# Attention probabilities of the second block: scaling by gate over denominator moved from VectorE to ScalarE, one step later

## The chip, the cores and the metric

One core of one Trainium2 chip runs the whole program. The metric is the time of one execution in microseconds (us) of device time; lower is better. The engines are TensorE (PE, with its weight loads shown apart as PEld), VectorE (DVE), ScalarE (ACT), GpSimd (POOL) and SyncE (SP). Each runs its own instructions in a fixed order and waits on semaphores for the others.

## What is computed

Two transformer blocks, one after the other, on 512 tokens of width 1024 in float32. The change lies in the second one, a sparse-attention mixer with 16 heads of 64 and three gated branches. Two of them, "selected" and "window", are the `br` 0 and 1 of the code. With 512 tokens both are ordinary causal attention with a bias by distance:

```
gates = sigmoid(g)                      # one per token, branch and head
logits = q @ k.T * dh ** -0.5 + bias    # (head, query, key)
p = masked_softmax(logits, dist >= 0)
o = p @ v
y = sum over branches of gates * o * silu(z)
...
h = x + rms_norm(y @ w_out)
```

So each row of probabilities may be multiplied by gate / denominator before it meets the values: both factors are one number per query and head.

## The kernel before, in words

All large products are made of three float32r products (high times high, low times high, high times low); weights are split into a high part by ScalarE (`wh`, line 172) and a low part by VectorE or, in the last part of the program, by GpSimd (`wl`, line 174).

The attention of the second block (function `attention`, about 960 to 1330 us of the span) has 128 steps: 8 pairs of heads, 2 branches, 2 heads of the pair, 4 blocks `tb` of 128 queries. Step k does this for its head and block, with n = 128, 256, 384 or 512 keys:

- `scores` (lines 1173 to 1182): PE makes the scores S in one of two PSUM banks that take turns (`sc`, banks 2 and 3). VectorE adds the bias in place and finds the row's extreme `nm` (line 1176). ScalarE takes the exponential into P, 128xn in SBUF, and sums it into `rd` (line 1180). VectorE takes the reciprocal of `rd` (line 1181) and multiplies P by `rd` and by the gate column in `gn`, in place (line 1182; the trace shows it as L295, the helper `ts`).
- `flip`, three steps later (`LAG` is 2): PE transposes P's blocks (line 1195) into one of two PSUM banks (`tp`, banks 4 and 5); ScalarE copies out the high part (`ptall`, line 1198), VectorE the low part (line 1199, shown as L301, the helper `tt`).
- `mix`, after every second flip and two steps later: PE multiplies by the values (line 1211); at a head's end ScalarE and VectorE move the sum out (`t`, lines 1217 and 1218).

P has one buffer for each `tb`, so step k+4 writes the buffer that step k's flip has read. Between these parts, `fill.run` issues pieces of other work on PE: the projections of keys, queries and of z (lines 341 to 343), and the compressed branch, whose 64 additions F_ on VectorE (line 910, shown as L301) fall in the first 100 us. `ns` sets how much by a budget of estimated PE time.

The order of instructions on PE and GpSimd is the program's (`manual_schedule`). On VectorE and ScalarE a scheduler sets the order when the program is built, by its own estimates of when each instruction can start.

Of the kernel before, what the change touches and what calls it, by code (L numbers as in the profile page):

```python
# [10 lines left out]
AF = mybir.ActivationFunctionType  # L11
OP = mybir.AluOpType
# [241 lines left out]
def tile_blocks(ctx, tc, x, xt, wts, prm, cst, table, post_g, w2k, w2v, out):  # L254
    nc = tc.nc
    v, s, g, pe, sy = nc.vector, nc.scalar, nc.gpsimd, nc.tensor, nc.sync
# [31 lines left out]
    def small(shape, name, bufs=2):  # L288
        return glob.tile(shape, F32, name=name, tag=name, bufs=bufs)

    def ts(out_, in_, s1, s2=None, op0=OP.mult, op1=None, eng=None):
        if s2 is None:
            (eng or v).tensor_scalar(out_, in_, s1, None, op0)
        else:
            (eng or v).tensor_scalar(out_, in_, s1, s2, op0, op1)  # L295
# [4 lines left out]
    def tt(out_, a, b, op=OP.mult, eng=None):  # L300
        (eng or v).tensor_tensor(out_, a, b, op)  # L301
# [478 lines left out]
    def nsa(x2, ssq2):  # L780
# [4 lines left out]
        with ExitStack() as pts:  # L785
# [46 lines left out]
            gn = pn.tile([128, 4, 48], F32, name="gn")  # L832
# [196 lines left out]
            def load_near(gq):  # L1029
                P = glob.tile([128, 16, 32], F32, name="Pc", tag="rb", bufs=1)  # L1030
                sy.dma_start(P.rearrange("p (t r) c -> p t r c", t=4), cb_d[:, :, 4 * gq:4 * gq + 4, :])
                pct["p", gq] = P

            def cmp_scores(gq, half):
                P = pct["p", gq]
                S = mx()
                used[0] = opened[0]
                for i in range(2):
                    for r in range(4):
                        t0 = 256 * half + 128 * i  # L1040
                        pe.matmul(S[:, 256 * i + 64 * r:256 * i + 64 * r + 64], qst[4 * gq + r][:, t0:t0 + 128],
                                  kc[:, gq].rearrange("p a b -> p (a b)"), start=True, stop=True)
                S4 = S.rearrange("p (a l b) -> p a l b", l=2, b=32)
                Ph = P[:, 8 * half:8 * half + 8, :]
                for l in range(2):
                    tt(Ph, S4[:, :, l, :], Ph, OP.add)

            def cmp_shift(gq):
                P = pct["p", gq]
                mns = small([128, 16], "mns")  # L1050
                v.tensor_reduce(mns, P, AX.X, OP.min)
                tt(P, P, mns[:, :, None].to_broadcast([128, 16, 32]), OP.subtract)
# [108 lines left out]
            class Unit:  # L1161
# [5 lines left out]
                def scores(self, tb):  # L1167
                    h, br = self.h, self.br
                    kh, kl = kst[h // 4, br]
                    n = 128 * tb + 128  # L1170
                    S = sc()
                    q = qst[h][:, 128 * tb:128 * tb + 128]
                    pe.matmul(S[:, 0:n], q, kh[:, 0:n], start=True, stop=False)
                    pe.matmul(S[:, 0:n], q, kl[:, 0:n], start=False, stop=True)
                    nm = small([128, 1], "nm", 4)
                    v.tensor_tensor_reduce(S[:, 0:n], S[:, 0:n], self.bt[:, h % 2, 512 - n:512], 1.0,  # L1176
                                           -NEG, OP.add, OP.min, nm)
                    P = pt.tile([128, n], F32, name="P", tag=f"P{tb}", bufs=1)
                    rd = small([128, 1], "rd", 4)
                    latest[0] = s.activation(P[:, 0:n], S[:, 0:n], AF.Exp, bias=nm, scale=-1.0, accum_out=rd)  # L1180
                    v.reciprocal(rd, rd)
                    ts(P[:, 0:n], P[:, 0:n], rd, gn[:, tb, 16 * br + 16 + h:16 * br + 17 + h], OP.mult, OP.mult)
                    self.P[tb] = P

                def flip(self, tb):
                    n = 128 * tb + 128
                    half, i = divmod(tb, 2)
                    if i == 0:
                        self.PT[half] = (ptall[:, turn[0], 0], ptall[:, turn[0], 1])
                        turn[0] = 1 - turn[0]  # L1190
                    PTh, PTl = self.PT[half]
                    P = self.P.pop(tb)
                    pst = tp()
                    for sb in range(tb + 1):
                        pe.transpose(pst[:, 128 * sb:128 * sb + 128], P[:, 128 * sb:128 * sb + 128], ident)  # L1195
                    src = pst[:, 0:n].rearrange("p (a b) -> p a b", b=128)
                    hi = PTh[:, 0:tb + 1, 128 * i:128 * i + 128]
                    s.copy(hi, src)
                    tt(PTl[:, 0:tb + 1, 128 * i:128 * i + 128], src, hi.bitcast(F32), OP.subtract)
# [18 lines left out]
                        tt(self.t1[a, :], self.t1[a, :], o[b, :], OP.add)  # L1218

            def attention(fill):  # L1220
                pend_flip, pend_mix = [], []
                steps = 128
                tick = [0]
                for p in range(1, 8):
                    fill.add(combine(p), 15600.0)
                    if p == 2:
                        fill.add(queries(6), 5200.0)
                    if p == 3:
                        fill.add(keys(3), 5200.0)
                    if p == 4:  # L1230
                        fill.add(queries(7), 5200.0)

                def mixes(limit=MLAG):
                    if len(pend_mix) > 0 and (tick[0] >= pend_mix[0][2] + limit):
                        u, half, _ = pend_mix.pop(0)
                        u.mix(half)
                        if u.h % 2 == 1 and u.br == 1 and half == 1:
                            attended(u.h // 2, u.ots)

                def flips(limit):  # L1240
                    if len(pend_flip) > limit:
                        u, tb = pend_flip.pop(0)
                        u.flip(tb)
                        if tb % 2 == 1:
                            return [(u, tb // 2, tick[0])]
                    return []

                bts = []
                bt2 = [pt.tile([128, 2, 512], F32, name="bt", tag=f"bt{i}", bufs=1) for i in range(2)]
                for bt in bt2:  # L1250
                    v.memset(bt[:, :, 0:256], 0.0)

                def load_bias(p):
                    bt = bt2[p % 2]
                    base = bt_d[2 * p:2 * p + 2]
                    sy.dma_start(bt[:, :, 256:512], bass.AP(tensor=base.tensor, offset=base.offset + 127,
                                                            ap=[[383, 128], [128 * 384, 2], [1, 256]]))
                    bts.append(bt)

                load_bias(0)  # L1260
                for p in range(8):
                    while p >= 2 and not {(p - 2, 1), (p - 2, 2)} <= joined:
                        fill.ticks += 1
                        assert fill._job() or fill._step() or fill.ticks < 9999
                    while (p // 2, 1) not in kst or 2 * p + 1 not in qst:
                        assert fill._step()
                    bt = bts.pop(0)
                    ots = []
                    for br in range(2):
                        t1 = pt.tile([128, T], F32, name="t1", tag="ot", bufs=4)  # L1270
                        ots.append(t1)
                        for e in range(2):
                            u = Unit(2 * p + e, br, bt, t1)
                            u.ots = ots
                            for tb in range(4):
                                steps -= 1
                                tick[0] += 1
                                ns = FILL if p < 2 else fill.left / (steps + TAIL)
                                u.scores(tb)
                                fill.run(ns / 2)  # L1280
                                new = flips(LAG)
                                fill.run(ns / 2)
                                mixes()
                                pend_mix += new
                                pend_flip.append((u, tb))
                            if br == 0 and e == 1 and p < 7:
                                load_bias(p + 1)
                while pend_flip or pend_mix:
                    tick[0] += 1
                    new = flips(0)  # L1290
                    fill.run(ns)
                    mixes()
                    pend_mix += new
# [114 lines left out]
```

## Time and profile before

| | |
|---|---|
| median of 3 runs | 1399.81 us (1399.77 to 1400.01) |
| the profiled execution | 1398.81 us, its span 1397.1 us |
| PE busy | 1337.3 us (96%) |
| VectorE busy | 808.5 us (58%) |
| ScalarE busy | 650.6 us (47%) |
| GpSimd busy | 261.2 us (19%) |
| mean granted clock of PE | 0.99 of full speed |

The shares are means over stages that differ. In the rows below a line such as L295 is a line of the kernel, often a helper's, `out<-in` names the tiles, and an engine's idle time is put down to the instruction that released it. "Busy" of PE contains modelled ends, so a busy PE is not PE at its peak.

### The profile page before, as it was taken

The page shows a single profiled execution, that of the slowest core. Times are in us where ns is not written, and L with a number is a line of the kernel's source. Part 1 is how long each engine was busy: PE and PEld are TensorE (multiplying, and loading weights), DVE is VectorE, ACT ScalarE, POOL GpSimd, SP SyncE. Part 2 cuts the span into 40 slices and gives each one's busy share as a digit, 9 for nine tenths or more (in the row PEclk, how much of TensorE's full clock was granted, in tenths as well). Part 3 has the DMA queues.
Part 4 walks back from the last instruction along what each step waited for, and adds up shares of the span by engine and source line. Part 5 has one row for each costly group of instructions (what it writes and reads, how often), then busy time and mean ns, then how long its engine had stood idle before and what let it go on. Part 6 is the DMA issues. An engine that isn't in the chain of part 4 may idle for free.

```text
span 1397.1 us, 17790 instructions
## 1 busy us (share of the span) xinstructions
PE 1337.3 (96%) x6622; PEld 1090.3 (78%) x6622; DVE 808.5 (58%) x1596; ACT 650.6 (47%) x1273; POOL 261.2 (19%) x230
## 2 busy tenths in 40 slices
PE   9999999999999999989999999899788999999897
PEld 7977787778786888868888888788677878777776
DVE  4678535556667535232233323455988998988823
ACT  6577624443434325341135422254446656665522
POOL 0022101111101000000000000134536242333352
PEclk9999999999999999999999999999999999999999
DMA  7411121213131414843333323314223122121132
GB/s 232 137 46 47 61 91 61 91 49 103 46 106 46 154 57 142 110 166 92 100 94 93 104 91 121 125 50 130 75 71 106 54 61 61 53 68 46 55 121 76
DMA packets 42039, 125.31 MB, mean 90 GB/s; under 512 B 4528, under 2 KB 11232, under 8 KB 41696
## 3 DMA queue, kind: packets, MB, share of 16 engines
q1 hardware_dynamic: 41952, 124.17, 29.4%
q8 instruction: 52, 0.85, 0.2%
q14 instruction: 35, 0.29, 0.1%
HBM read 115.77 MB, written 8.39 MB: 89 GB/s over the span
## 4 chain that ended last, share of the span: by engine, by line
PE 59%; DVE 16%; issue 15%; ACT 6%; POOL 2%; DMA 1%; SPq 0%; POOLq 0%; DVEq 0%; ACTq 0%
PE b L375 9%; PE b L374 9%; PE b L376 9%; PE b L341 8%; PE b L343 8%; PE b L342 8%; DVE P L295 4%; DVE b L1176 2%; DVE ptall L301 2%; ACT wh L172 1%; PE b L827 1%; ACT P L1180 1%; PE b L1211 1%; PE b L544 1%; PE b L1195 1%
## 5 line engine op out<-in xcount | busy, mean ns | idle before, releaser
L172 ACT CAST wh<-wr 128x1024 fp32r<-128x1024 f32 (+3 forms) x204 | 207.6, 1020 | 385.9 <-PE b L376 222.7
L341 PE MATMUL b<-ah,wh 128*128 128x512 f32 x808 | 330.5, 409 | 6.3 <-ACT wh L172 5.9
L174 DVE TENSOR_TENSOR wl<-wr,wh 128x1024 fp32r<-128x1024 f32 (+2 forms) x142 | 169.2, 1194 | 281.1 <-ACT wh L172 280.7
L343 PE MATMUL b<-ah,wl 128*128 128x512 f32 x808 | 318.9, 395 | 0.6 <-DVE wl L174 0.5
L342 PE MATMUL b<-al,wh 128*128 128x512 f32 x808 | 318.2, 394 | 0.0
L343 PEld LDWEIGHTS b<-ah,wl 128*128 128x128 f32 x808 | 152.8, 189 | 35.4 <-DVE wl L174 1.8
L341 PEld LDWEIGHTS b<-ah,wh 128*128 128x128 f32 x808 | 153.0, 189 | 34.3 <-ACT wh L172 6.7
L174 POOL TENSOR_TENSOR wl<-wr,wh 128x1024 fp32r<-128x1024 f32 (+1 forms) x62 | 143.6, 2320 | 159.0 <-ACT wh L172 149.4
L342 PEld LDWEIGHTS b<-al,wh 128*128 128x128 f32 x808 | 153.4, 190 | 24.5 <-issue 0.5
L374 PE MATMUL b<-wh,ah 128*128 128x512 f32 (+3 forms) x352 | 125.9, 359 | 1.0 <-ACT wh L172 0.6
L376 PE MATMUL b<-wh,al 128*128 128x512 f32 (+3 forms) x352 | 125.5, 357 | 0.1
L375 PE MATMUL b<-wl,ah 128*128 128x512 f32 (+3 forms) x352 | 125.3, 356 | 0.1
L1180 ACT ACTIVATE P<-b,nm 128x128 f32<-128x128 f32 (+3 forms) x128 | 67.5, 528 | 104.8 <-DVE nm L1176 102.6
L375 PE MATMUL b<-wl,hh 128*128 128x512 f32 x256 | 102.1, 399 | 0.0
L374 PE MATMUL b<-wh,hh 128*128 128x512 f32 x256 | 100.9, 394 | 0.0
L376 PE MATMUL b<-wh,hl 128*128 128x512 f32 x256 | 100.4, 392 | 0.0
L295 DVE TENSOR_SCALAR P<-P,rd,gn 128x128 f32<-128x128 f32 (+3 forms) x128 | 93.4, 730 | 2.5
L301 POOL TENSOR_TENSOR rsr<-rsm,mhalf 128x2 f32<-128x2 f32 (+1 forms) x3 | 2.4, 802 | 476.6 <-DVE rsm L295 476.6
L374 PEld LDWEIGHTS b<-wh,ah 128*128 128x128 f32 x352 | 66.2, 188 | 9.8 <-ACT wh L172 0.9
L376 PEld LDWEIGHTS b<-wh,al 128*128 128x128 f32 x352 | 66.4, 189 | 8.8 <-DVE al L298 0.5
L375 PEld LDWEIGHTS b<-wl,ah 128*128 128x128 f32 x352 | 66.4, 189 | 8.4 <-DVE wl L174 0.5
L1195 PE MATMUL b<-ident,P 128*128 128x128 f32 x320 | 56.7, 275 | 12.7 <-DVE ptall L301 10.4
(286 smaller groups left out, 2213.5 us busy)
## 6 DMA issues: line engine op xcount, KB each, us to landing
wr<-in_wts_dram SPq DMA_DIRECT2D x188, 512.0 KB, 3.5
bt_d<-tr SPq DMA_DIRECT2D x4, 768.0 KB, 20.5
wr<-in_wts_dram SPq DMA_DIRECT2D x8, 280.0 KB, 2.6
xk<-in_xt_dram SPq DMA_DIRECT2D x8, 256.0 KB, 3.8
xn<-in_x_dram SPq DMA_DIRECT2D x4, 512.0 KB, 4.9
xbig<-in_x_dram SPq DMA_DIRECT2D x1, 2048.0 KB, 9.9
x_d<-xbig SPq DMA_DIRECT2D x8, 256.0 KB, 2.9
bt<-bt_d SPq DMA_DIRECT2D x8, 256.0 KB, 2.7
```

What stands on the lines that cost most here:

```text
L172: nc.scalar.copy(hi, raw)
L174: eng.tensor_tensor(lo, raw, hi.bitcast(F32), OP.subtract)
L295: (eng or v).tensor_scalar(out_, in_, s1, s2, op0, op1)
L301: (eng or v).tensor_tensor(out_, a, b, op)
L341: pe.matmul(o, a, ah, start=(kt == 0), stop=False)
L342: pe.matmul(o, a, al, start=False, stop=False)
L343: pe.matmul(o, b, ah, start=False, stop=(kt == KT - 1))
L374: pe.matmul(o, ah[:, tsl], a, start=(kk == 0 and k == 0), stop=False)
L375: pe.matmul(o, ah[:, tsl], b, start=False, stop=False)
L376: W.last = pe.matmul(o, al[:, tsl], a, start=False, stop=end)
L1180: latest[0] = s.activation(P[:, 0:n], S[:, 0:n], AF.Exp, bias=nm, scale=-1.0, accum_out=rd)
L1195: pe.transpose(pst[:, 128 * sb:128 * sb + 128], P[:, 128 * sb:128 * sb + 128], ident)
```

## The change

VectorE no longer multiplies P. It makes a column `gs` = gate times reciprocal (128x1) instead. The multiplication of P by `gs` becomes a ScalarE activation (Identity with a column as its scale, in place, 128xn), the new method `scale`, which the program issues one step later, right behind the next step's `scores`. After the last step one more call takes the one that is left. PE's, GpSimd's and SyncE's rows are the same, in the same order.

```diff
--- before.py
+++ after.py
@@ -1178,9 +1178,15 @@
                     P = pt.tile([128, n], F32, name="P", tag=f"P{tb}", bufs=1)
                     rd = small([128, 1], "rd", 4)
                     latest[0] = s.activation(P[:, 0:n], S[:, 0:n], AF.Exp, bias=nm, scale=-1.0, accum_out=rd)
+                    gs = small([128, 1], "gs", 4)
                     v.reciprocal(rd, rd)
-                    ts(P[:, 0:n], P[:, 0:n], rd, gn[:, tb, 16 * br + 16 + h:16 * br + 17 + h], OP.mult, OP.mult)
-                    self.P[tb] = P
+                    tt(gs, gn[:, tb, 16 * br + 16 + h:16 * br + 17 + h], rd)
+                    self.P[tb] = (P, gs)
+
+                def scale(self, tb):
+                    P, gs = self.P[tb]
+                    n = 128 * tb + 128
+                    s.activation(P[:, 0:n], P[:, 0:n], AF.Identity, scale=gs)
 
                 def flip(self, tb):
                     n = 128 * tb + 128
@@ -1189,7 +1195,7 @@
                         self.PT[half] = (ptall[:, turn[0], 0], ptall[:, turn[0], 1])
                         turn[0] = 1 - turn[0]
                     PTh, PTl = self.PT[half]
-                    P = self.P.pop(tb)
+                    P = self.P.pop(tb)[0]
                     pst = tp()
                     for sb in range(tb + 1):
                         pe.transpose(pst[:, 128 * sb:128 * sb + 128], P[:, 128 * sb:128 * sb + 128], ident)
@@ -1218,7 +1224,7 @@
                         tt(self.t1[a, :], self.t1[a, :], o[b, :], OP.add)
 
             def attention(fill):
-                pend_flip, pend_mix = [], []
+                pend_flip, pend_mix, pend_scale = [], [], []
                 steps = 128
                 tick = [0]
                 for p in range(1, 8):
@@ -1244,6 +1250,11 @@
                         if tb % 2 == 1:
                             return [(u, tb // 2, tick[0])]
                     return []
+
+                def scales():
+                    if pend_scale:
+                        u, tb = pend_scale.pop(0)
+                        u.scale(tb)
 
                 bts = []
                 bt2 = [pt.tile([128, 2, 512], F32, name="bt", tag=f"bt{i}", bufs=1) for i in range(2)]
@@ -1277,6 +1288,8 @@
                                 tick[0] += 1
                                 ns = FILL if p < 2 else fill.left / (steps + TAIL)
                                 u.scores(tb)
+                                scales()
+                                pend_scale.append((u, tb))
                                 fill.run(ns / 2)
                                 new = flips(LAG)
                                 fill.run(ns / 2)
@@ -1285,6 +1298,7 @@
                                 pend_flip.append((u, tb))
                             if br == 0 and e == 1 and p < 7:
                                 load_bias(p + 1)
+                scales()
                 while pend_flip or pend_mix:
                     tick[0] += 1
                     new = flips(0)
```

The scheduler places the new rows. Two places show it. The first is VectorE in the stretch of the F_ additions, from the z product of the fill on: `ISA b,nm` is the biased scores with their extreme, `RECIPROCAL rd` and the row behind it end a step. Before:

```order
L298 SCALAR_TENSOR_TENSOR z<-z,b_7701 128x512
L301 TENSOR_TENSOR ptall<-b_7842,ptall 128x128
L1181 RECIPROCAL rd<-rd 128x1
L1176 ISA b_7851,nm<-b_7851,bt 128x128
L1176 ISA nm 128x1
L295 TENSOR_SCALAR P<-P,rd,gn 128x512
L1181 RECIPROCAL rd<-rd 128x1
L295 TENSOR_SCALAR P<-P,rd,gn 128x128
L301 TENSOR_TENSOR ptall<-b_7880,ptall 128x2x128
L1176 ISA b_7901,nm<-b_7901,bt 128x256
L1176 ISA nm 128x1
```

and with the change:

```order
L298 SCALAR_TENSOR_TENSOR z<-z,b_7710 128x512
L1176 ISA b_7866,nm<-b_7866,bt 128x128
L1176 ISA nm 128x1
L1182 RECIPROCAL rd<-rd 128x1
L301 TENSOR_TENSOR ptall<-b_7857,ptall 128x128
L301 TENSOR_TENSOR gs<-gn,rd 128x1
L1182 RECIPROCAL rd<-rd 128x1
L301 TENSOR_TENSOR gs<-gn,rd 128x1
L301 TENSOR_TENSOR ptall<-b_7897,ptall 128x2x128
L1176 ISA b_7918,nm<-b_7918,bt 128x256
```

The large TENSOR_SCALAR rows on P are gone, one-column rows on `gs` stand in their place, and the biased scores of the next step have moved ahead of a `ptall` row.

The second is ScalarE in the middle of the attention, behind the third exponential of the compressed branch (`Pc`): `P,rd<-b,nm` is a step's exponential, `CAST ptall` the high part of a flip, `P<-P,gs` the new scaling. Before:

```order
L1056 ACTIVATE Pc<-Pc 128x512
L1217 COPY t_10228<-b_10444 64x512
L1180 ACTIVATE P,rd<-b_10513,nm 128x256
L1198 CAST ptall<-b_10526 128x3x128
L172 CAST wh<-wr 128x1024
L1180 ACTIVATE P,rd<-b_10532,nm 128x384
L987 ACTIVATE z<-b_10430 128x512
L1198 CAST ptall<-b_10547 128x4x128
L1198 CAST ptall<-b_10588 128x128
L1180 ACTIVATE P,rd<-b_10572,nm 128x512
```

and with the change:

```order
L1056 ACTIVATE Pc<-Pc 128x512
L1189 ACTIVATE P<-P,gs 128x128
L1223 COPY t_10387<-b_10617 64x512
L1180 ACTIVATE P,rd<-b_10690,nm 128x256
L1204 CAST ptall<-b_10705 128x3x128
L1189 ACTIVATE P<-P,gs 128x256
L172 CAST wh<-wr 128x1024
L987 ACTIVATE z<-b_10603 128x512
L1180 ACTIVATE P,rd<-b_10711,nm 128x384
L1204 CAST ptall<-b_10728 128x4x128
L1189 ACTIVATE P<-P,gs 128x384
L1180 ACTIVATE P,rd<-b_10753,nm 128x512
```

Each exponential is now followed by the scaling of its own step within a few rows, and that scaling stands ahead of the next step's exponential; so it is over the whole attention in 99 of the 128 steps.

## Rows read from the trace of the kernel before

**Rows 1.** The page's costliest groups: line, engine, operation, out<-in xcount | busy us, mean ns | idle before.
```profile
L295 DVE TENSOR_SCALAR P<-P,rd,gn 128x128 f32<-128x128 f32 (+3 forms) x128 | 93.4, 730 | 2.5
```

**Rows 2.** Busy us of each engine by stage, then PEclk, DMA share, GB/s; last the three together.
```profile
960.00:1060.00 100.00, 85.57 (x476) 72.57 (x475) 88.83 (x202) 50.29 (x115) 50.26 (x33) 0.97 0.29 88
1060.00:1110.00 50.00, 46.89 (x258) 39.15 (x258) 44.99 (x114) 30.94 (x79) 19.58 (x10) 0.97 0.26 80
1110.00:1330.00 220.00, 207.15 (x1198) 171.59 (x1198) 197.11 (x532) 133.13 (x346) 75.75 (x42) 1.00 0.18 55
sum 370.00, PE 339.61 PEld 283.30 DVE 330.93 ACT 214.36 POOL 145.59; mean PE 113.20 PEld 94.43 DVE 110.31 ACT 71.45 POOL 48.53
```

**Rows 3.** Waits in 960:1330: who waited <- for whom: us in all, times, longest us.
```profile
ACT P L1180 <- DVE nm L1176: 102.6, 72, 3.9
PEld b L1195 <- DVE ptall L301: 15.7, 15, 2.3
PEld b L1173 <- ACT P L1180: 14.4, 12, 3.1
```

**Rows 4.** The ten-us windows of 960:1320 with DVE below 8.8: first, and sum of 14.
```profile
960.00:970.00 10.00, 9.10 (x47) 7.59 (x46) 8.18 (x18) 5.44 (x13) 4.51 (x2) 1.00 0.49 158
sum 140.00, PE 133.44 PEld 111.26 DVE 118.79 ACT 82.85 POOL 67.32; mean PE 9.53 PEld 7.95 DVE 8.49 ACT 5.92 POOL 4.81
```

**Rows 5.** The ten-us windows of 960:1320 with DVE above 9.2: first two, and sum of 13.
```profile
980.00:990.00 10.00, 7.10 (x42) 5.68 (x40) 9.68 (x24) 2.30 (x5) 2.98 (x6) 1.00 0.17 52
990.00:1000.00 10.00, 5.56 (x29) 5.15 (x30) 9.71 (x21) 5.75 (x12) 5.11 (x5) 0.86 0.00 0
sum 130.00, PE 113.30 PEld 94.83 DVE 123.99 ACT 70.64 POOL 49.06; mean PE 8.72 PEld 7.29 DVE 9.54 ACT 5.43 POOL 3.77
```

**Rows 6.** Groups on DVE in 960:1110 alone.
```profile
L295 DVE TENSOR_SCALAR P<-P,rd,gn 128x128 f32<-128x128 f32 (+3 forms) x40 | 35.5, 887 | 0.8
L301 DVE TENSOR_TENSOR F__7705<-kv,pr 64x124 f32<-64x124 f32 x8 | 4.6, 581 | 0.5 <-ACT kv L893 0.4
```

**Rows 7.** Timeline of DVE's scalings in 1150:1165, start us, us; last POOL's operation beside the slow one.
```profile
1158.81 0.35 DVE L295 TENSOR_SCALAR P<-P,rd,gn 128x128 f32<-128x128 f32 x1
1154.49 0.41 DVE L295 TENSOR_SCALAR P<-P,rd,gn 128x256 f32<-128x256 f32 x1
1155.37 0.48 DVE L295 TENSOR_SCALAR P<-P,rd,gn 128x384 f32<-128x384 f32 x1
1158.16 0.55 DVE L295 TENSOR_SCALAR P<-P,rd,gn 128x512 f32<-128x512 f32 x1
1161.52 1.45 DVE L295 TENSOR_SCALAR P<-P,rd,gn 128x256 f32<-128x256 f32 x1
1160.43 2.39 POOL L174 TENSOR_TENSOR wl<-wr,wh 128x1024 fp32r<-128x1024 f32 x1 [6.77 <-ACT wh L172]
```

**Rows 8.** Shapes of the scaling kept apart, 960:1330.
```profile
L295 DVE TENSOR_SCALAR P<-P,rd,gn 128x512 f32<-128x512 f32 x32 | 25.7, 804 | 0.4
L295 DVE TENSOR_SCALAR P<-P,rd,gn 128x128 f32<-128x128 f32 x32 | 22.6, 705 | 0.5
```

**Rows 9.** The tile rgc: duration ns min/median/max; timeline: its longest, and POOL beside it.
```profile
L301 DVE TENSOR_TENSOR rgc<-rgc,gn x4: 158/170/1067, 1100.3 to 1312.8; 128x16 f32<-128x16 f32 x4
...
1312.83 1.07 DVE L301 TENSOR_TENSOR rgc<-rgc,gn 128x16 f32<-128x16 f32 x1
1312.51 1.35 POOL L301 TENSOR_TENSOR z<-z 128x512 f32<-128x512 f32 x1
```

**Rows 10.** ScalarE's Identity activations with a column as scale, SBUF to SBUF, shapes apart, 0:960.
```profile
L560 ACT ACTIVATE spare<-spare,mnr 128x128 f32<-128x128 f32 x32 | 10.2, 392 | 2.8 <-DVE mnr L301 2.7
L496 ACT ACTIVATE y<-xp,pr 128x512 f32<-128x512 f32 x8 | 5.7, 718 | 0.6 <-DVE AT L301 0.4
```

## Prediction

> **What bounds the kernel now.** I read the views in this order: the page's groups for the operation that goes, busy time by stage, the waits, windows of ten microseconds, then single instructions. The scaling of P costs VectorE 93.4 us in 128 instructions of 730 ns, nearly all with no idle time before them: the engine goes from one instruction straight to the next [rows 1]. By stage, VectorE is busy 330.9 of 370 us of the attention (89%), ScalarE 214.4 (58%) and PE 339.6 (92%) [rows 2]. So PE sets the end, but it stands idle for 30.4 us there, and that is the most that a change off PE can give back directly. The idle time is uneven: 17.5 us in the first 150 us (960 to 1110) and 12.9 us in the 220 us after it.
>
> The waits say who is late. ScalarE's exponential waits 102.6 us, in 72 of 128 steps, for the row extreme from VectorE; PE's weight loads wait 14.4 us in 12 steps for an exponential to free the scores' bank and 15.7 us in 15 steps for VectorE's low part of a flip to free the transposes' bank [rows 3]. All these chains pass through VectorE's queue. The windows agree: in the 14 with VectorE below 8.8 of 10 us, PE is busy 133.4 of 140 us (95.3%), in the 13 above 9.2 it is 113.3 of 130 us (87.2%) [rows 4, 5]. The worst two lie where the F_ additions crowd VectorE, PE at 7.1 and 5.6 of 10 us [rows 5].
>
> **What goes and what comes, on VectorE.** Away go the 93.4 us [rows 1]. In come 128 products of two 128x1 columns. No such row exists; the nearest is the gating of the compressed branch, also a product of two SBUF operands with 16 columns: 158 ns at least, 170 median, 1067 at most in four instructions [rows 9]. Two ends: 158 ns each (20 us in all), or as long as the scaling it replaces, 730 ns (93.4 us, no relief). I take the mean of the four, (158 + 170 + 170 + 1067)/4 = 391 ns, the middle two being near their median; that is 50 us in all. The long one is no accident, see the second rival. VectorE then has 330.9 - 93.4 + 50 = 287.5 us of work, 78% of the stage. In the crowded first 150 us, 40 scalings take 887 ns each, 35.5 us together [rows 6]; at 391 ns that falls by 19.8 us, against 17.5 us of PE idle.
>
> **On ScalarE.** In come 128 activations with a column as scale, SBUF to SBUF. The same form stands in the first block: 392 ns for 128 columns, 718 for 512 [rows 10]; between them in a straight line 501 and 609. The sum is 32 x (392 + 501 + 609 + 718) = 71.0 us, mean 555 ns. ScalarE goes from 214.4 to 285.4 us, 77%. No table is loaded anew, the changed order has as many such rows as before. What covers this work is the 155.6 us in which ScalarE idles; what can be hurt is whatever now queues behind it. In 99 of 128 steps the scaling stands ahead of the next exponential and waits for `gs`, which waits for the exponential before it. So each step now crosses between the engines twice. PE's scores wait for that next exponential.
>
> By the unhindered rows the multiplication is dearer on ScalarE: VectorE's four shapes take 0.35, 0.41, 0.48 and 0.55 us [rows 7], 57 us in all, against 71. The Trainium skill, "ScalarE: Activation LUTs", section "Rules for kernel authors", says to give multiplications to VectorE rather than ScalarE; by that rule the change adds 14 us of engine time and the sum would be slower by up to as much. The stage decides otherwise for me: the engine that is relieved is 89% busy, the one that is loaded 58%.
>
> **What PE gets.** VectorE's 78% is lower than every window shown, so I take PE's share from the low windows and no better: 95.3% instead of 91.8% of 370 us, which is 13.0 us. By stage that is 17.5 - 0.047 x 150 = 10.4 us in the crowded 150 us and 12.9 - 0.047 x 220 = 2.5 us after it. The ends are nothing and the whole 30.4 us. Against it I set ScalarE's queue: of the 12 steps in which PE waits for an exponential, half go on waiting, each longer by a scaling, 6 x 0.555 = 3.3 us (ends: nothing, 12 x 0.555 = 6.7 us). At the very end the last scaling is on the path once, 718 + 158 instead of 550 ns, 0.3 us. P's buffers cost nothing: a buffer is written again four steps later, the flip comes three steps later, and the scaling must be over some two steps of 370/128 = 2.9 us earlier. DMA, GpSimd's and PE's orders don't move. The granted clock is 0.97 in the first 150 us, where PE stands longest, and 1.00 after [rows 2]; less standing may give back up to 0.03 x 150 = 4.5 us. I count none, since the F_ additions, 4.6 us for one group of eight [rows 6], stay and make the longest stands.
>
> Sum: -13.0 + 3.3 + 0.3 = -9.4 us. The profiled execution took 1398.8 us (span 1397.1 and 1.7 around it), the median of the runs is 1.0 above that; so 1389.4 for a profiled execution and **1390.4** for the median. All times below are medians, from 1399.8.
>
> **Rivals.**
>
> 1. *More than the low windows show.* VectorE falls below any window seen, and all 30.4 us of idle go: 1369.4. For it: the late stage has windows with PE at 10 of 10 beside VectorE at 8.2 to 8.5. Against it: F_ stays, and ScalarE fills up.
>
> 2. *The new column waits for GpSimd as P did.* One scaling of 256 columns took 1.45 us instead of 0.41; it ended at 1162.97 us, beside GpSimd's subtraction that ended at 1162.82 [rows 7]. The 1067 ns product ended at 1313.90, GpSimd's add at 1313.86 [rows 9]. So a column of two SBUF operands is held up too. If each `gs` carries the excess of the 128-column scaling over its best, 705 - 350 = 355 ns [rows 7, 8], it costs 158 + 355 = 513 ns, 65.7 us in all; VectorE's relief is 27.7 us instead of 43.4, and the gain 13.0 x 27.7/43.4 = 8.3 us: 1399.8 - 8.3 + 3.6 = 1395.1. The Trainium skill, "SBUF — State Buffer", section "SBUF: two separate sides", states this as an exclusive lock: a VectorE operation with two SBUF inputs waits for a GpSimd operation that reads SBUF to end; the trace agrees with the two pairs above.
>
> 3. *The crowded stretches stay VectorE's.* F_ is not touched; if the 10.4 us of the first 150 us don't come and only the 2.5 us of the late stage do, then -2.5 + 3.6 = +1.1: 1400.9, no difference.
>
> 4. *ScalarE's queue becomes the bound: slower.* The scaling ahead of the next exponential, waiting for VectorE's `gs`, holds up exponentials and flips' copies. If PE's waits of today stay as long, now ended by ScalarE, and the 12 for exponentials grow by a scaling each, that is +6.7 us: 1406.5. It decides once ScalarE's share between 1110 and 1330 us, now 133.1/220 = 61%, with its new work and its waits for `gs` reaches what VectorE has there now, 197.1/220 = 90%. Its busy time alone should come to some 80%: 88 of the 128 steps lie there, 88 x 0.555 = 49 us more.
>
> **How the numbers follow.** About 0.2%, 2.8 us, is what a measurement of this kernel can tell from no change. Chances: forecast 0.48, rival 1 0.08, rival 2 0.14, rival 3 0.13, rival 4 0.17. Faster: 0.48 + 0.08 + 0.14 = 0.70; same 0.13; slower 0.17. The forecast's own bounds are 1384 (the clock's 4.5 us and half of ScalarE's 3.3 us fall its way) and 1396. The range reaches to rivals 2 and 3 and part of 1 and 4: 1378 to 1404.
>
> **What would show it.** Right: the page has the 730 ns group gone, 128 Identity activations of some 555 ns, products on `gs` near 0.4 us in the mean; VectorE near 78% and ScalarE near 77% of the stage; waits of the exponential for `nm` well below 102.6 us; PE's idle time in the attention near 21 us, with most of the fall before 1110. Wrong, towards rival 2: `gs` at 0.5 us or above. Towards rival 4: new waits of ScalarE's scaling for `gs`, and PE's waits for the exponential above 14.4 us. Towards rival 1: those waits nearly gone and the stage shorter by 25 us or more.

## The result, and the profile after

The changed kernel is slower: 1419.4 us in the median of four runs (1412.8 to 1422.1) against 1399.8 before, a ratio of 1.0136 (95% interval 1.0100 to 1.0171). That is +19.6 us where -9.4 was forecast, and outside the range of 1378 to 1404. The page shown here is of the execution of 1412.8 us, the fastest of the four; it shows 14 of the 20 us.

Busy time of each engine over the whole span, from the page after:

```profile
PE 1339.3 (95%) x6622; PEld 1090.3 (77%) x6622; DVE 783.3 (56%) x1596; ACT 712.7 (51%) x1401; POOL 259.5 (18%) x230
```

VectorE has 25 us less than before and ScalarE 62 us more; PE has the same instructions. By stage (busy us of PE, PEld, DVE, ACT, POOL, each with its count; PEclk, DMA share, GB/s), the attention now ending near 1344 us:

```profile
960.00:1060.00 100.00, 83.13 (x449) 69.48 (x449) 79.50 (x196) 58.48 (x133) 45.84 (x32) 0.95 0.26 79
1060.00:1110.00 50.00, 46.08 (x259) 38.73 (x258) 41.64 (x111) 37.56 (x90) 22.05 (x12) 0.97 0.28 86
1110.00:1330.00 220.00, 200.36 (x1157) 164.81 (x1156) 175.91 (x518) 170.14 (x420) 73.36 (x42) 1.00 0.17 52
...
sum 384.00, PE 341.17 PEld 282.51 DVE 305.41 ACT 276.18 POOL 143.61; mean PE 85.29 PEld 70.63 DVE 76.35 ACT 69.04 POOL 35.90
```

Beside [rows 2] the work moved as it was meant to: VectorE from 330.9 to 305.4 us, 80% of the 384 us, ScalarE from 214.4 to 276.2 us. PE's idle time rose, from 30.4 of 370 us to 42.8 of 384 us. The loss lies in all stages: PE is busy 83.1 instead of 85.6 us in the first 100, and 200.4 instead of 207.2 us from 1110 to 1330. Two groups of PE hold most of the idle time (busy us, mean ns | idle before): the flips' transposes, which need a free transposes' bank, and the scores, which need a free scores' bank. Before:

```profile
L1195 PE MATMUL b<-ident,P 128*128 128x128 f32 x320 | 56.7, 275 | 12.7 <-DVE ptall L301 10.4 <-DVE rd L1181 2.1
L1173 PE MATMUL b<-kh,q 128*128 128x128 f32 (+3 forms) x128 | 44.9, 351 | 11.9 <-ACT P L1180 10.7 <-DVE vst L301 0.9
```

and with the change:

```profile
L1201 PE MATMUL b<-ident,P 128*128 128x128 f32 x320 | 57.4, 277 | 20.7 <-DVE ptall L301 14.9 <-DVE rd L1182 5.8
L1173 PE MATMUL b<-kh,q 128*128 128x128 f32 (+3 forms) x128 | 44.8, 350 | 14.0 <-ACT P L1180 13.1 <-DVE vst L301 0.9
```

Of the 12.4 us that PE lost, 8.0 lie ahead of the transposes and 2.1 ahead of the scores.

The waits in 960:1344 (who waited <- for whom: us in all, times, longest us):

```profile
ACT P L1189 <- DVE gs L301: 51.2, 66, 2.6
DVE rd L1182 <- ACT P L1180: 36.2, 58, 1.5
ACT P L1180 <- DVE nm L1176: 23.0, 33, 3.2
...
PEld b L1173 <- ACT P L1180: 17.5, 15, 3.4
DVE ptall L301 <- ACT ptall L1204: 16.5, 20, 1.8
PEld b L1201 <- issue: 16.3, 16, 3.0
...
DVE t L301 <- ACT t L1223: 9.1, 17, 2.3
```

Two of these waits in the kernel before, in 960:1330:

```profile
DVE rd L1181 <- ACT P L1180: 23.8, 43, 1.4
...
DVE t L301 <- ACT t L1217: 2.5, 2, 1.9
```

Beside [rows 3], the exponential's wait for `nm` fell from 102.6 to 23.0 us, as foreseen. In its place stand 51.2 us in which the scaling waits for `gs`, and VectorE in turn waits more for ScalarE: for an exponential before the reciprocal (36.2 us, 23.8 before), for a flip's copy (16.5 us, 0.5 before), for the head's sum (9.1 us, 2.5 before). Part of VectorE's relief has turned into waiting. These waits of VectorE are not by themselves the loss: the faster version with `gs` from one tensor, below, has 37.6, 16.9 and 11.9 us of them. The waits of PE's weight loads for an exponential rose from 14.4 to 17.5 us. The 16.3 us of "issue" ahead of transposes have no releaser named; one of them, below, ends with a low part on VectorE.

The tiles of the new instructions (ns min/median/max):

```profile
L301 DVE TENSOR_TENSOR gs<-gn,rd x128: 135/160/2386, 966.7 to 1339.8; 128x1 f32<-128x1 f32 x128
L1189 ACT ACTIVATE P<-P,gs x128: 387/564/743, 966.9 to 1340.2; 128x128 f32<-128x128 f32 x32, 128x256 f32<-128x256 f32 x32, 128x384 f32<-128x384 f32 x32, 128x512 f32<-128x512 f32 x32
```

```profile
L1189 ACT ACTIVATE P<-P,gs 128x128 f32<-128x128 f32 (+3 forms) x128 | 71.9, 564 | 56.0 <-DVE gs L301 51.2 <-DVE rd L1182 3.7
...
L301 DVE TENSOR_TENSOR gs<-gn,rd 128x1 f32<-128x1 f32 x128 | 65.1, 509 | 2.9
```

The scaling costs 564 ns, as estimated (555). The column `gs` costs 160 ns in the median and 509 in the mean, up to 2386. A stretch of the timeline shows what such a column does (start us, us, idle before):

```profile
1251.49 0.57 ACT L1180 ACTIVATE P<-b,nm 128x384 f32<-128x384 f32 x1
...
1251.66 2.38 POOL L174 TENSOR_TENSOR wl<-wr,wh 128x1024 fp32r<-128x1024 f32 x1 [3.84 <-PE b L343]
...
1252.19 0.16 DVE L1182 RECIPROCAL rd<-rd 128x1 f32<-128x1 f32 x1 [1.15 <-ACT P L1180]
...
1252.39 1.67 DVE L301 TENSOR_TENSOR gs<-gn,rd 128x1 f32<-128x1 f32 x1
...
1253.98 0.69 DVE L1176 CUSTOM_DVE_ANT_0 b<-b,bt 128x512 f32<-128x512 f32 x1
...
1254.16 0.61 ACT L1189 ACTIVATE P<-P,gs 128x384 f32<-128x384 f32 x1 [1.04 <-DVE gs L301]
...
1254.76 0.69 ACT L1180 ACTIVATE P<-b,nm 128x512 f32<-128x512 f32 x1
1255.19 0.68 DVE L301 TENSOR_TENSOR ptall<-b,ptall 128x512 fp32r<-128x512 f32 x1
...
1256.02 0.41 PE L1201 MATMUL b<-ident,P 128*128 128x128 f32 x2 [2.63 <-DVE rd L1182]
```

VectorE first waits 1.15 us for ScalarE's exponential. Then `gs`, one column, takes 1.67 us and ends at 1254.06, beside GpSimd's subtraction that ends at 1254.04. ScalarE has waited 1.04 us for it, and the next exponential (128x512) stands behind the scaling and starts at 1254.76. On VectorE the next scores, a product of z and a flip's low part stand behind `gs`; the low part ends at 1255.87, and PE's transposes start at 1256.02 after 2.63 us of standing. The view names the reciprocal `rd`, which ended at about the same time; by the program the transposes need P, which was scaled by 1250.65, and the bank that this low part frees. One late column has held up VectorE, ScalarE and PE. At its median the column takes 0.16 us, so it was 1.51 us late; by this chain that is the larger part of PE's 2.63 us, and not all of it.

The stretch is typical of the late columns. Over the trace 43 of the 128 took more than 300 ns, 51.8 us together. Each of the 43 started while an operation of GpSimd ran, 29 times the subtraction `wl`, and ended 14 to 23 ns after that operation. Of the other 85, 163 ns at most, two started beside GpSimd.

### The profile page after: what moved, and what is told of

It reads as the page before. It is cut to its first block, busy times and chain, and to the rows that moved or that the text cites. A ratio compares the mean times of both kernels' runs of the same rounds, so it can differ in the third digit from the quotient of the medians.

```text
span 1411.1 us, 17933 instructions
## 1 busy us (share of the span) xinstructions
PE 1339.3 (95%) x6622; PEld 1090.3 (77%) x6622; DVE 783.3 (56%) x1596; ACT 712.7 (51%) x1401; POOL 259.5 (18%) x230
## 4 chain that ended last, share of the span: by engine, by line
PE 55%; issue 16%; DVE 14%; ACT 11%; POOL 3%; DMA 0%; POOLq 0%; ACTq 0%; SPq 0%; DVEq 0%
PE b L376 9%; PE b L375 9%; PE b L374 9%; PE b L341 7%; PE b L343 7%; PE b L342 7%; DVE gs L301 3%; ACT P L1180 3%; ACT wh L172 2%; ACT P L1189 2%; DVE ptall L301 2%; DVE b L1176 2%; PE b L827 1%; POOL wl L174 1%; PE b L544 1%
## 5 line engine op out<-in xcount | busy, mean ns | idle before, releaser
L1189 ACT ACTIVATE P<-P,gs 128x128 f32<-128x128 f32 (+3 forms) x128 | 71.9, 564 | 56.0 <-DVE gs L301 51.2
L1201 PE MATMUL b<-ident,P 128*128 128x128 f32 x320 | 57.4, 277 | 20.7 <-DVE ptall L301 14.9
## 6 DMA issues: line engine op xcount, KB each, us to landing
bt_d<-tr SPq DMA_DIRECT2D x4, 768.0 KB, 20.5
```

What stands on the lines that cost most here:

```text
L1189: s.activation(P[:, 0:n], P[:, 0:n], AF.Identity, scale=gs)
```

## The experiments

Theory A: the held-up `gs`, through those who wait for it. Theory B: the order on ScalarE, the scaling ahead of the next exponential. Theory C: 72 us more work on ScalarE by itself. Differences are taken to the kernel before as it was timed for each run (medians 1398.9 to 1399.8), unless two versions are named. Each profile is of one execution.

**The scaling behind the next exponential.**

```diff
-                    s.activation(P[:, 0:n], P[:, 0:n], AF.Identity, scale=gs)
+                    with tc.issue_after(latest[0].ins):
+                        s.activation(P[:, 0:n], P[:, 0:n], AF.Identity, scale=gs)
```

> The changed kernel, but ScalarE's scaling of a step stands behind the next step's exponential (1 of 128 ahead of it instead of 99). Theory A (a column product gs that waits for GpSimd stalls VectorE, and ScalarE with it): gs stays near 509 ns, the time stays at 1410 to 1420 us. Theory B (the order on ScalarE, a scaling that waits for its own step's gs ahead of the next exponential): ScalarE's waits for gs fall from 51.2 us to under 15, the time falls to 1390 to 1402. Theory C (72 us more work on ScalarE by itself): no change, 1410 to 1420.

Measured: 1410.0 us, ratio 1.0077 (1.0059 to 1.0095). Waits and groups of this run in 960:1345:

```profile
ACT P L1180 <- DVE nm L1176: 57.1, 58, 3.6
...
ACT P L1190 <- DVE gs L301: 4.4, 5, 1.5
```

```profile
L301 DVE TENSOR_TENSOR gs<-gn,rd 128x1 f32<-128x1 f32 x128 | 65.8, 514 | 3.2
```

ScalarE's wait for `gs` is all but gone (4.4 us), yet the time fell by only 9.4 us against the changed kernel, and `gs` is held up as long as before. That is what theory B gave for the wait but not for the time, and the lower edge of what theories A and C gave for the time. The order is a part, not the whole.

**`gs` from one tensor.**

```diff
-                    tt(gs, gn[:, tb, 16 * br + 16 + h:16 * br + 17 + h], rd)
+                    ts(gs, gn[:, tb, 16 * br + 16 + h:16 * br + 17 + h], rd)
```

> The changed kernel, with gs made by a tensor_scalar (the gate column as its only tensor, the reciprocal as a scalar column) instead of a product of two tensors. Theory A: gs falls from 509 ns to 160 to 220, VectorE is relieved by some 40 us more, the time falls to 1388 to 1402 us. Theory B: gs falls too, but the time stays above 1408, since the order stays. Theory C: 1410 to 1420. If the new form is held up by GpSimd as well, gs stays near 500 ns and the run says nothing between the theories.

Measured: 1391.1 us, ratio 0.9944 (0.9925 to 0.9963). The new column (ns min/median/max):

```profile
L293 DVE TENSOR_SCALAR gs<-gn,rd x128: 180/214/217, 966.7 to 1317.5; 128x1 f32<-128x1 f32 x128
```

```profile
ACT P L1189 <- DVE gs L293: 26.5, 53, 1.6
```

The column takes 211 ns in the mean and never more than 217, though 51 of the 128 started while an operation of GpSimd ran; ScalarE's wait for it halves. This one call takes 28.3 us away and turns the slower kernel into one faster than before. The order on ScalarE is nearly the same (98 of 128 steps), and so is that of VectorE's other rows. Theory A's forecast is met; B and C, which gave 1408 and more, cannot be the whole.

**Both edits.** The two diffs above together.

> Both edits together: the scaling behind the next exponential, and gs from one tensor. If A or B holds alone, the time is that of the better of the two runs before within 3 us; if both hold, it is below each of them by more than 3 us, at 1383 to 1395, and below the kernel before. Theory C: still 1408 or more.

Measured: 1389.9 us, ratio 0.9936 (0.9916 to 0.9956), the fastest of the versions that compute all of it, though within the interval of the run before. With `gs` on time the order hardly matters, so theory B holds only where `gs` is late.

**ScalarE's load alone, not held to the steps.** The kernel before, with a tile of its own:

```diff
                                 u.scores(tb)
+                                s.activation(junk[:, 0:128 * tb + 128], junk[:, 0:128 * tb + 128], AF.Identity,
+                                             scale=ones[:, 0:1])
```

> The kernel before, plus 128 ScalarE Identity activations of the same shapes with a constant column as scale, on a tile of their own, issued where the scaling is issued; nothing depends on them and they depend on nothing. Adds some 71 us of ScalarE work and no wait. Theory C: 1408 us or more. Theories A and B: at most 1404.

Measured: 1417.0 us, ratio 1.0125 (1.0102 to 1.0148). It says little: nothing held the activations back, and the scheduler put all of them between 897 and 1072 us (tile `junk`, first and last start):

```profile
L1282 ACT ACTIVATE junk<-junk,ones x128: 388/580/747, 896.6 to 1071.6; 128x128 f32<-128x128 f32 x32, 128x256 f32<-128x256 f32 x32, 128x384 f32<-128x384 f32 x32, 128x512 f32<-128x512 f32 x32
```

**VectorE's relief alone.** The kernel before without the line of the multiplication (1182).

> The kernel before without VectorE's multiplication of P, and nothing in its place; it leaves gate and denominator out of the probabilities of both branches. It shows what VectorE's relief alone is worth. The prediction's step took 13.0 us for a relief to 78% of the stage; this relief goes to 64%. If that step holds: 1375 to 1387 us. If VectorE wasn't what held PE (theory C, ScalarE's own work decides): 1395 or more.

Measured: 1379.7 us, ratio 0.9860 (0.9840 to 0.9880), that is -19.5 us. Sum row of the same stage:

```profile
sum 355.00, PE 340.23 PEld 289.73 DVE 256.04 ACT 219.27 POOL 147.90; mean PE 113.41 PEld 96.58 DVE 85.35 ACT 73.09 POOL 49.30
```

PE is busy 340.2 of 355 us (95.8%) with VectorE at 72%. PE's idle time ahead of the transposes falls from 12.7 to 1.8 us. VectorE was what held PE, and the step of the prediction from VectorE's load to PE's share stands.

**The held-up column without the scaling.**

```diff
-                    s.activation(P[:, 0:n], P[:, 0:n], AF.Identity, scale=gs)
+                    pass
```

> The changed kernel without ScalarE's scaling: gs is made as a product of two tensors, still held up by GpSimd, and used by nothing; it leaves gate and denominator out. Theory A as first put (a late gs hurts because ScalarE waits for it): the time falls to 1385 to 1395 us, though gs stays near 500 ns. If the lost VectorE time alone hurts: 1400 or more. The rest up to the changed kernel's 1412 to 1422 is then what ScalarE's scaling and its waits cost.

Measured: 1393.2 us, ratio 0.9956 (0.9941 to 0.9970): -6.0 us, with `gs` at 474 ns. Of the 19.5 us that the relief is worth, the column gives 13.5 back on VectorE itself, with nothing waiting for it.

**ScalarE's load alone, spread over the steps.** The same load, but each activation behind its step's exponential:

```diff
+                                with tc.issue_after(latest[0].ins):
+                                    s.activation(junk[:, 0:128 * tb + 128], junk[:, 0:128 * tb + 128], AF.Identity,
+                                                 scale=ones[:, 0:1])
```

> The earlier run with 128 free-standing ScalarE activations let the scheduler put them all between 897 and 1072 us, so its 1417 us say nothing of a load spread over the steps. Here each stands right behind its step's exponential, and nothing depends on it. Theory C (72 us more work on ScalarE costs by itself, beside a VectorE at 89%): 1408 or more. Theories A and B: at most 1404.

Measured: 1410.6 us, ratio 1.0078 (1.0057 to 1.0099): +11.4 us. Groups in 955:1345 (busy us, mean ns):

```profile
L295 DVE TENSOR_SCALAR P<-P,rd,gn 128x128 f32<-128x128 f32 (+3 forms) x128 | 100.1, 782 | 3.2
L1283 ACT ACTIVATE junk<-junk,ones 128x128 f32<-128x128 f32 (+3 forms) x128 | 71.2, 556 | 0.0
...
L1195 PE MATMUL b<-ident,P 128*128 128x128 f32 x320 | 57.7, 278 | 21.3 <-DVE ptall L301 15.0 <-DVE rd L1181 6.1
```

Work of 71 us on ScalarE that waits for nothing and that nothing waits for costs 11 us, though ScalarE was idle for 155.6 us of the stage before. What it delays are the flips' copies: ScalarE's high part starts 2.26 us after the flip's last transpose in the mean, 1.66 us in the kernel before, and PE's idle time ahead of the transposes rises from 12.7 to 21.3 us, while that ahead of the scores does not rise (10.7 against 11.9). Theory C holds for this part. One rival is left: the scheduler also set the other rows anew, and about a sixth of VectorE's rows of the attention stand elsewhere than before; the run does not part that from the load.

**VectorE's lost time, spread evenly.** The version with `gs` from one tensor, and behind each `gs`:

```diff
+                    with tc.issue_after(made.ins):
+                        v.reciprocal(pad, pad)
```

> The changed kernel with gs from one tensor (1391 us), plus one more VectorE instruction right behind each gs: a reciprocal of 128x28 on a tile of its own, estimated at 300 ns from the rows of 1 and 16 columns (160 and 238 ns), so that VectorE loses as much time as the held-up gs lost (509 - 211 = 298 ns), but evenly, and not ahead of ScalarE's scaling. If lost VectorE time is what made the change slow: 1408 to 1420. If it is the wait of ScalarE for a late gs, or the unevenness of it (up to 2.4 us at once): 1390 to 1400.

Measured: 1394.8 us, ratio 0.9966 (0.9954 to 0.9977). The padding (busy us, mean ns):

```profile
L1187 DVE RECIPROCAL pad<-pad 128x28 f32<-128x28 f32 x128 | 40.7, 318 | 0.0
```

VectorE loses 40.7 us here, more than the 38.1 us that the held-up column lost (65.1 against 27.0), and it costs 3.7 us against 28.3. So it is not the amount of lost time that hurts but when it comes: up to 2.4 us at once, and ahead of the scaling on which ScalarE's next work hangs. This run takes away both at once and does not part them.

**The changed kernel's loads without the dependence.** `gs` as in the changed kernel, unused; the activations of the spread load in place of the scaling.

> The changed kernel with gs still a product of two tensors, but ScalarE's 128 activations take a constant column on a tile of their own, each right behind its step's exponential, so that they wait for nothing; gate and denominator are left out. If loads add up and the rest of the changed kernel's 1419 us is ScalarE waiting for the late gs: 1393.2 (gs alone) + 11.4 (ScalarE's load alone) = 1404.6, that is 1401 to 1409. If the two loads hurt each other without that wait: 1414 or more.

Measured: 1398.1 us, ratio 0.9997 (0.9983 to 1.0012), no difference from the kernel before. Groups in 955:1345:

```profile
L1294 ACT ACTIVATE junk<-junk,ones 128x128 f32<-128x128 f32 (+3 forms) x128 | 71.3, 557 | 0.0
...
L301 DVE TENSOR_TENSOR gs<-gn,rd 128x1 f32<-128x1 f32 x128 | 67.2, 525 | 3.1
...
L1201 PE MATMUL b<-ident,P 128*128 128x128 f32 x320 | 57.3, 277 | 17.5 <-DVE ptall L301 11.9 <-DVE rd L1182 5.5
```

The same work on both engines and a column held up as much (525 ns) make 1398.1 us; the changed kernel takes 1419.4. The 21.3 us between them (20.5 as differences to before) are the price of the dependence, the scaling that waits for `gs`, together with the orders that the scheduler makes of it: about a tenth of VectorE's rows of the attention stand elsewhere in the two. That the loads would add up (1404.6 us) was wrong by 6.5 us in the good direction, so the two loads don't hurt each other beyond it.

**The multiplication kept on VectorE, read from PSUM.**

```diff
-                    latest[0] = s.activation(P[:, 0:n], S[:, 0:n], AF.Exp, bias=nm, scale=-1.0, accum_out=rd)
+                    latest[0] = s.activation(S[:, 0:n], S[:, 0:n], AF.Exp, bias=nm, scale=-1.0, accum_out=rd)
...
-                    ts(P[:, 0:n], P[:, 0:n], rd, gn[:, tb, 16 * br + 16 + h:16 * br + 17 + h], OP.mult, OP.mult)
+                    ts(P[:, 0:n], S[:, 0:n], rd, gn[:, tb, 16 * br + 16 + h:16 * br + 17 + h], OP.mult, OP.mult)
```

> The kernel before, with the exponential written back in place into the scores' PSUM bank and VectorE's multiplication reading it there and writing P; ScalarE gets no new work. If VectorE's multiplication is held up by GpSimd only in its SBUF to SBUF form, it takes some 0.29 to 0.70 us by width (mean near 0.49, as the flips' low parts from PSUM do) instead of 0.73, at most 0.75 us ever, and VectorE is relieved by 30 us: 1385 to 1396 us. Against it: the scores' bank stays taken until the multiplication ends, so PE's waits for it may grow: then 1399 or more.

Measured: 1401.4 us, ratio 1.0012 (0.9991 to 1.0033), no difference. The tile P and the waits of this run:

```profile
L295 DVE TENSOR_SCALAR P<-b,rd,gn x128: 398/604/814, 968.4 to 1329.2; 128x128 f32<-128x128 f32 x32, 128x256 f32<-128x256 f32 x32, 128x384 f32<-128x384 f32 x32, 128x512 f32<-128x512 f32 x32
```

```profile
PEld b L1173 <- DVE P L295: 34.2, 30, 6.0
```

From PSUM the multiplication is not held up: 814 ns at most where it was 3344. But it takes 605 ns in the mean, more than the 490 expected, and PE's waits for the scores' bank rise from 14.4 to 34.2 us, now for the multiplication. One wait was traded for another, as the expectation's second case had it.

**The head's sum copied by VectorE**, on top of both edits.

```diff
-                        s.copy(self.t1[a, :], o[a, :])
+                        v.tensor_copy(self.t1[a, :], o[a, :])
```

> The run with both edits (1389.9 us), with the copy of a head's sum moved from ScalarE to VectorE: 31 copies, 18 us off ScalarE and some 21 us onto VectorE, and one crossing between the engines less. If ScalarE's load is what is left of the price of the move (11 us for 72 us of it), it gives 1 to 4 us: 1386 to 1389. If both engines are alike by now: 1389 to 1392.

Measured: 1390.7 us, ratio 0.9942 (0.9923 to 0.9961); against the 1389.9 us without it no difference. Shifting this piece between the two engines brings nothing.

## Why the prediction was wrong

The way from the kernel before to the changed one, in the runs' medians as differences to before; beside them PE's idle time ahead of the scores and the transposes, from one profiled execution of each (us):

| version | time | ahead of scores | ahead of transposes |
|---|---|---|---|
| before | 0 | 11.9 | 12.7 |
| VectorE relieved | -19.5 | 11.3 | 1.8 |
| with the held-up column | -6.0 | 11.7 | 9.0 |
| with ScalarE's load as well | -0.9 | 8.2 | 17.5 |
| with the dependence (the change) | +19.6 | 14.0 | 20.7 |
| the change, `gs` from one tensor | -8.2 | 11.7 | 8.3 |

Against the sum of the prediction: the relief with the held-up column gave -6.0 us where -13.0 stood, ScalarE's load cost 5.1 us where 3.3 + 0.3 stood, and for the dependence, 20.5 us, the sum has no term. The three misses, 7.0, 1.5 and 20.5 us, are the 29.0 us between -9.4 and +19.6.

1. **What bounds the kernel**: right. PE waits for VectorE's queue, and taking the multiplication away gives 19.5 us, between the 13.0 us taken and the 30.4 us of all idle time.

2. **What comes on VectorE**: too low. The column was put at 391 ns, the mean of four instructions; it is 509 ns, and the second rival's 513 ns was the right price. That rival priced the relief with this column at 8.3 us; the run with the column and no scaling gave 6.0 us. The Trainium skill's statement in "SBUF — State Buffer", section "SBUF: two separate sides", that a VectorE operation with two SBUF inputs waits for a GpSimd operation that reads SBUF, if that one began first, agrees with the 43 late columns. It does not cover the first of the rival's two pairs: the scaling of P has one tensor and two scalar columns, and was held up all the same. The new column as a tensor and one scalar column was not (217 ns at most).

3. **What comes on ScalarE**: the instruction was priced rightly (564 ns against 555), its effect was not. The step "of the 12 steps in which PE waits for an exponential, half go on waiting, each longer by a scaling, 6 x 0.555 = 3.3 us (ends: nothing, 12 x 0.555 = 6.7 us)" is the one that failed. The load by itself costs 11.4 us beside VectorE's old load and 4.8 us beside the relieved one with its late column (1393.2 to 1398.1; 5.1 as differences to before), and not at that place: what it adds to PE's idle time lies ahead of the transposes. And the step priced the scaling only by its length, not by its wait. The hold-up by GpSimd and the second crossing were set down as two rivals, each with a price of its own; they work together. A column that is 2 us late used to be a multiplication that delayed VectorE alone, while ScalarE had its own work to go on with; now ScalarE stops too, 51.2 us in all, and the exponentials and copies behind the scaling come later. This wait is what the sum left out; with the orders that come of it, the change costs 21.3 us more than its loads.

4. **The rivals**: the fourth had the right sign and the right engine, with 6.7 us instead of 19.6. It looked for the growth in PE's waits for an exponential, and these grew by 3.1 us; most of the loss is ahead of the transposes. Its mark was met: between 1110 and 1330 us ScalarE's busy time is 170.1 us, and with the waits for `gs` and `rd` of its scaling and exponential there, 29.9 + 2.2 + 1.4 + 0.2 us, it is occupied for 203.8 of 220 us (93%), above the 90% named. Its waits:

```profile
ACT P L1189 <- DVE gs L301: 29.9, 42, 2.2
ACT P L1180 <- DVE nm L1176: 13.9, 25, 1.1
ACT P L1180 <- DVE gs L301: 2.2, 3, 1.1
ACT P L1189 <- DVE rd L1182: 1.4, 1, 1.4
...
ACT P L1180 <- DVE rd L1182: 0.2, 1, 0.2
```

5. **The rule against the change**, from the Trainium skill, "ScalarE: Activation LUTs", section "Rules for kernel authors" (multiplications to VectorE): it was set aside for the engines' shares. As a verdict on the move it is not borne out, since the same move with the column from one tensor gains 8.2 us. That ScalarE's idle time is not free is a lesson of another run, the spread load.

The flip's wait for the scaling is not part of the 21.3 us. In the profile after, each scaling ended 0.85 us or more before its transposes began, and in all 19 flips ahead of which PE stood for more than 0.1 us it was the low part freeing the bank that ended last, not the scaling. So the price runs through the queues of ScalarE and VectorE. What stays open is how the 21.3 us divide between ScalarE's wait for `gs` and the order of the rows. With the scaling behind the next exponential ScalarE's wait for `gs` is 4.4 us and the time 1410.0 us: 9.4 us of the 21.3 are gone and 11.9 are left, with PE idle for 20.4 us ahead of the transposes. No run keeps every other row in its place.

## What to carry to other kernels

When work moves from one engine to another, price the new dependence and not only the new busy time: ask what stands behind the first instruction that waits, and how late its input can be at worst, not in the mean. A tiny instruction can be held up for the length of another engine's large one, here a column of 128 numbers that took up to 2.4 us; look for another form of it before anything else is moved, and read in the trace whether that form is held up too. Two rivals that lie on one chain are not to be priced apart.

## What had not been expected of the hardware

A product of two columns takes 160 ns in the median and up to 2386 ns beside GpSimd's operations; the same product as a tensor_scalar, the second column as its scalar, takes 180 to 217 ns. A tensor_scalar is not safe as such: the scaling of P in the kernel before was one too, of 128 to 512 columns from SBUF to SBUF, and took up to 3344 ns; all 31 that took more than 900 ns started while an operation of GpSimd ran and ended 0.08 to 0.29 us after the end of one. Work of 71 us on an engine that idled for 155.6 of 370 us cost 11.4 us though nothing depended on it. The multiplication with two scalar columns from PSUM takes 398 to 814 ns, where the flips' low parts of the same shapes from PSUM take 283 to 680 ns in the mean of each shape.
